# A mixture-of-experts decoder in which the experts' scatters add their rows to a copy of the residual in DRAM

## The chip, the cores and the metric

The kernel runs on one core of a Trainium2 chip. The metric is the device time of one execution in microseconds (us). Names used throughout: PE is TensorE (matmuls), PEld its weight loads, DVE is VectorE, ACT is ScalarE, POOL is GpSimd, SP is SyncE, which here only issues DMAs. POOL issues the indirect DMAs (gathers and scatters by a list of row numbers); all other transfers stand in one queue issued by SP, in program order.

## What is computed

Two decoder layers over 512 tokens of width 1024. A layer mixes tokens (two kinds of attention, unchanged here), normalizes, sends each token through 2 of 16 experts, adds, and normalizes again:

```python
x = layer_norm(DN_ALPHA * x + mix, ln1_g[l], ln1_b[l])            # "x1" below
ffn = grouped_moe(x, w_router, router_bias, exp_w_gate[l], exp_w_up[l], exp_w_down[l])
x = layer_norm(DN_ALPHA * x + ffn, ln2_g[l], ln2_b[l])

# in grouped_moe: combine[n, e] is the token's weight for expert e, zero for 14 of the 16
for e in range(N_EXPERTS):
    h = jax.nn.silu(xf @ exp_w_gate[e]) * (xf @ exp_w_up[e])
    y = y + combine[:, e:e + 1] * (h @ exp_w_down[e])
```

All is float32. `DN_ALPHA` is 4 ** 0.25, written `ALPHA` in the kernel. `layer_norm` adds `LN_EPS` to the variance.

## The kernel before

**Matmuls.** Tokens lie in four tiles of 128 rows (`NT` = 4). Each operand is split into a high and a low part (a CAST on ACT, then a subtraction on DVE, `split`, L484 and L495), and a product is three matmuls (`mm3`, L447). An expert reads 12 weight tiles of 128x1024 (512 KB each), so it has 12 such splits and 72 matmuls of 512 columns.

**Who sets the order.** Operations are recorded with a duration and dependencies, and `plan` lays them out on a model of the engines: it decides in which order each engine gets its instructions, which of 48 slots of 4 KB per partition (kind "s") or 56 small slots (kind "m") each tile takes, and when SP issues loads. The order is then fixed in the program: an instruction that waits holds up all behind it on its engine, SP's DMAs included. The model lets a POOL transfer end 0.65 us and the bytes' time and 0.9 us after its issue.

**Routing.** For each token tile, `out_proj` forms the first LayerNorm's output x1 and stores it to DRAM (`x1d`). `route_tile` picks the two experts and writes two entries (token number, weight) by scatters into a table in DRAM (`tabd`, L1151), row r of expert e for its r-th token; the first choice carries the token number, the second the number plus 512. `route_end` reads the first 128 rows of every expert back (`tb`) and computes from it the rows to gather (`gi`: numbers of 512 and more less 512).

**Experts.** `moe` runs expert after expert: `prep` gathers the expert's rows of x1 (POOL, L1179) and transposes them, `gate_up` makes 48 matmuls, `down` 24, and `put_rows` (L1185) scatters the weighted result into `yd`, a DRAM tile of 1024 rows: first choices in rows 0 to 511, second choices in the rest, so every row is written once and no scatter waits for another. The last expert's rows go nowhere by scatter; zeros are scattered for them at the start (tile z, L1342) and its result (yo and lo, its high and low part) is added in the second LayerNorm by matmuls with a one-hot matrix (`oh`). `overflow` is a branch (L1203) that every engine meets once in a layer, and whose body runs only where an expert has over 128 tokens; in this data none has, and the trace has no instruction of the body. Between the condition and the code that follows stand three copies of the body, 108 matmuls on PE.

**End of the layer.** For each tile x1 is loaded from `x1d` and both halves from `yd` (12 loads of 512 KB), two DVE operations of 128x1024 form ALPHA*x1 + y0 + y1, and `ln2` adds the last expert in PSUM (a matmul with the identity, then two with `oh`), takes mean and variance (tile 0 on DVE, the others on ACT), normalizes on DVE, stores the tile and, in the first layer, transposes and splits it for the next layer's projections. Loads of weights that follow in the program (ln2's, the next layer's `w_idx` and `w_main`) may be issued from the middle of expert 13 on (`R.after = mark`).

Of the kernel before, what the change touches and what calls it, by code (L numbers as in the profile page):

```python
# [11 lines left out]
F = mybir.dt.float32  # L12
FR = mybir.dt.float32r
BF = mybir.dt.bfloat16
I32 = mybir.dt.int32
# [7 lines left out]
P = 128  # L23
# [68 lines left out]
class Recorder:  # L92
# [82 lines left out]
    def plan(self):  # L175
# [109 lines left out]
        while done < len(self.ops):  # L285
# [69 lines left out]
            elif e == "POOL" and o.nbytes:  # L355
# [3 lines left out]
                o.end = dma_free + 0.9  # L359
# [176 lines left out]
THROTTLE = 3  # L536
# [7 lines left out]
def build(tc, x0, xT0, w_idx, w_main, w_br, w_out, w_exp, bgate, idxg, idxb,  # L544
          ln1g, ln1b, ln2g, ln2b, wrt, rbias, ln1c, hconst, tab0, out):
    nc = tc.nc
    with ExitStack() as ctx:
# [3 lines left out]
                 "k": ctx.enter_context(tc.tile_pool(name="k", bufs=1)),  # L551
                 "p": ctx.enter_context(tc.tile_pool(name="p", bufs=1, space=PSUM)),
# [3 lines left out]
        yd = tc.dram_tile([2 * S, D], F, name="yd")  # L556
# [4 lines left out]
        R.COUNT = {"s": NSLOT, "m": NSMALL, "k": 1, "p": 4, "a": 4}  # L561
# [22 lines left out]
        nc.gpsimd.iota(tokid, pattern=[[P, NT], [S, 2]], base=0, channel_multiplier=1)  # L584
# [74 lines left out]
        def rstd_of(mv):  # L659
            v, r = sm([P, 1]), sm([P, 1])  # L660
            C.ts(v, mv[:, 1:2], LN_EPS, None, OP.add)
            C.pow(r, v, nhalf)
            return r
# [4 lines left out]
        def norm_of(mv, bs):  # L668
            C.v("bn_aggr", mv, bs, n=12)
            return rstd_of(mv)  # L670
# [357 lines left out]
        def out_proj(l, mts, pair, xres, xtok, rw, rsum, rcon):  # L1028
# [26 lines left out]
            for t in range(NT):  # L1055
# [16 lines left out]
                C.dma(x1d[ts, :], r, P * 4096, wtok=[f"x1{t}"])  # L1072
                yield t, r, sc, scored, o
# [19 lines left out]
        def route_tile(t, rt, sc, scored, sels, oh0, xacc):  # L1093
# [44 lines left out]
            o2, ri = sm([P, 2, NE]), sm([P, 2], I32)  # L1138
            C.tt(o2, oh, pr[:, None, :NE].to_broadcast([P, 2, NE]), OP.mult)
            C.v("reduce_max", ri, o2, axis=AX.X, n=2 * NE)  # L1140
            ent, o3, w2, rw = sm([P, 2, 2], I32), sm([P, 2, NE]), sm([P, 2]), sm([P, 2])
# [5 lines left out]
            last = C.ts(ent[:, :, 1:2].bitcast(F), w2[:, :, None], rw[:, 1:2], None, OP.mult)  # L1147
# [12 lines left out]
        scatters, table_writes, picks, later, puts, written = [], [], [], [], [], []  # L1160

        def route_end(sels):
# [6 lines left out]
            tb, gi, gl = sm([P, NE, 2], I32), sm([P, NE], I32), sm([P, 2], I32)  # L1169
            o = C.dma(tb, tabd[0:P * NE, :].rearrange("(r e) w -> r e w", e=NE), P * 160, rtok=["tab0"])  # L1170
            o.deps.update(table_writes)
            C.ts(gi, tb[:, :, 0], float(S), float(-S), OP.is_ge, OP.mult)
            C.tt(gi, gi, tb[:, :, 0], OP.add)
            C.ts(gl[:, 0:1], gi[:, NE - 1:NE], float(S - 1), None, OP.min)
            return tb, gi, gl, mci
# [7 lines left out]
        def put_rows(idx, src, l, wait=()):  # L1183
            def fn():
                s_ = nc.gpsimd.indirect_dma_start(out=yd, out_offset=IOA(ap=real(idx), axis=0), in_=real(src), in_offset=None,  # L1185
                                                  bounds_check=2 * S - 1, oob_is_err=False)
                for x in puts:
# [423 lines left out]
```

## Time and profile before

| | us |
|---|---|
| median of 3 runs | 1546.22 (1542.68 to 1550.23) |
| the profiled execution | 1544.22 |
| its span in the trace | 1542.5 |
| PE busy in the span | 1477.8 (96%) |
| DVE busy | 1268.0 (82%) |
| ACT busy | 896.6 (58%) |
| POOL busy | 128.4 (8%) |
| DMA, mean over the span | 203 GB/s |

The trace is to be read by stage. Layer 1 takes the first 750 us or so: attention to 360, output projection and routing to about 450, the experts to about 750; layer 2 repeats this. The views used are the busy times in chosen stretches, the timeline of one engine (with the idle time before an instruction and what ended it, in brackets), the waits, and the views of one line of the code.

### The profile page before, as it was taken

The page shows a single profiled execution, that of the slowest core. Times are in us where ns is not written, and L with a number is a line of the kernel's source. Part 1 is how long each engine was busy: PE and PEld are TensorE (multiplying, and loading weights), DVE is VectorE, ACT ScalarE, POOL GpSimd, SP SyncE. Part 2 cuts the span into 40 slices and gives each one's busy share as a digit, 9 for nine tenths or more (in the row PEclk, how much of TensorE's full clock was granted, in tenths as well). Part 3 has the DMA queues.
Part 4 walks back from the last instruction along what each step waited for, and adds up shares of the span by engine and source line. Part 5 has one row for each costly group of instructions (what it writes and reads, how often), then busy time and mean ns, then how long its engine had stood idle before and what let it go on. Part 6 is the DMA issues. An engine that isn't in the chain of part 4 may idle for free. (4 is left out here: it accounts for less than half of the span.)

```text
span 1542.5 us, 21103 instructions
## 1 busy us (share of the span) xinstructions
PE 1477.8 (96%) x7188; PEld 1177.3 (76%) x7188; DVE 1268.0 (82%) x2321; ACT 896.6 (58%) x1459; POOL 128.4 (8%) x131
## 2 busy tenths in 40 slices
PE   8999999999989999999799999999999899999985
PEld 7877777777867788888487777777778578877874
DVE  5699995877687999989875999867766889899987
ACT  4335543674147888888433455346841578878773
POOL 0000000000131211111010000000001311111100
PEclk9999999999999999999899999999999899999998
DMA  7222113118778899999712211221287789999993
GB/s 222 72 84 67 57 55 96 56 42 304 268 249 307 328 349 343 335 337 332 297 69 67 85 55 55 83 82 55 68 316 254 260 309 337 347 331 323 351 328 147
DMA packets 92708, 313.15 MB, mean 203 GB/s; under 512 B 15757, under 2 KB 15885, under 8 KB 92592
## 3 DMA queue, kind: packets, MB, share of 16 engines
q1 hardware_dynamic: 83152, 294.88, 54.6%
q0 software_dynamic: 9440, 16.83, 3.0%
q8 instruction: 60, 0.98, 0.3%
q14 instruction: 56, 0.46, 0.1%
HBM read 302.19 MB, written 25.31 MB: 212 GB/s over the span
## 5 line engine op out<-in xcount | busy, mean ns | idle before, releaser
L447 PE MATMUL p<-s,s 128*128 128x512 f32 (+1 forms) x5192 | 1267.1, 397 | 30.0 <-DVE s L495 25.0
L447 PEld LDWEIGHTS p<-s,s 128*128 128x128 f32 x5192 | 950.2, 190 | 240.2 <-DVE s L495 25.6
L495 DVE TENSOR_TENSOR s<-s,s 128x1024 fp32r<-128x1024 f32 (+3 forms) x534 | 621.2, 1196 | 140.2 <-ACT s L484 106.8
L484 ACT CAST s<-s 128x1024 fp32r<-128x1024 f32 (+2 forms) x526 | 515.7, 1030 | 200.9 <-PE p L447 130.6
L495 DVE TENSOR_TENSOR s<-a,s 128x256 fp32r<-128x256 f32 (+3 forms) x386 | 168.8, 480 | 43.9 <-ACT s L484 40.4
L484 ACT CAST s<-a 128x256 fp32r<-128x256 f32 (+2 forms) x354 | 126.2, 414 | 123.7 <-PE a L445 107.1
L445 PE MATMUL a<-ident,s 128*128 128x128 f32 x888 | 132.3, 277 | 12.4 <-DMA s<-x1d,m 7.1
L445 PEld LDWEIGHTS a<-ident,s 128*128 128x128 f32 x888 | 106.2, 142 | 43.6 <-DVE s L495 11.4
L523 POOL TENSOR_TENSOR m<-m,nhalf 128x1 f32<-128x1 f32 x24 | 17.8, 743 | 902.1 <-DVE m L495 902.1
L480 ACT ACTIVATE s<-a 128x512 f32<-128x512 f32 (+3 forms) x156 | 61.8, 450 | 47.1 <-PE a L447 28.0
L484 ACT COPY s<-a 64x512 f32<-64x512 f32 (+1 forms) x48 | 27.8, 583 | 97.2 <-PE a L445 45.9
L487 ACT ACTIVATE s<-p,m 128x512 f32<-128x512 f32 (+1 forms) x64 | 44.2, 690 | 53.5 <-PE p L447 49.3
L464 PE MATMUL a<-s,s 64*128 64x384 f32 (+3 forms) x456 | 67.4, 351 | 0.0
L1179 POOL DMA_INDIRECT s<-x1d,m x30 | 42.9, 1430 | 265.6 <-PE p L447 248.3
L1185 POOL DMA_INDIRECT yd<-s,m x32 | 46.1, 1440 | 209.6 <-ACT s L487 189.6
L447 PEld LDWEIGHTS a<-s,s 128*128 128x128 f32 x360 | 57.1, 188 | 7.8 <-issue 2.4
L447 PE MATMUL a<-s,s 128*128 128x324 f32 (+4 forms) x360 | 62.4, 321 | 0.2
L464 PEld LDWEIGHTS a<-s,s 64*128 64x128 f32 x456 | 41.3, 185 | 27.6 <-issue 20.0
L495 DVE MAX8 m<-s 128x8 f32<-128x256 f32 (+2 forms) x96 | 53.5, 557 | 1.8
L495 DVE MATCH_REPLACE8 s<-m,s 128x256 f32<-128x256 f32 (+2 forms) x96 | 52.1, 543 | 0.0
L495 DVE TENSOR_TENSOR_SCAN s<-s 128x128 f32<-128x128 f32 (+3 forms) x64 | 51.1, 814 | 0.1
L484 ACT CAST s<-p 128x512 fp32r<-128x512 f32 x48 | 27.9, 588 | 35.6 <-DVE p L495 19.8
(108 smaller groups left out, 650.6 us busy)
## 6 DMA issues: line engine op xcount, KB each, us to landing
s<-in_w_exp SPq DMA_DIRECT2D x384, 512.0 KB
s<-in_w_main SPq DMA_DIRECT2D x79, 512.0 KB
s<-in_w_br SPq DMA_DIRECT2D x16, 512.0 KB
s<-in_w_out SPq DMA_DIRECT2D x16, 512.0 KB
s<-yd SPq DMA_DIRECT2D x16, 512.0 KB
x1d<-s SPq DMA_DIRECT2D x8, 512.0 KB
s<-x1d SPq DMA_DIRECT2D x8, 512.0 KB
s<-in_w_idx SPq DMA_DIRECT2D x8, 324.0 KB
```

The source lines that it names most:

```text
L445: self.nc.tensor.transpose(o, real(transpose[0]), transpose[1])
L447: self.nc.tensor.matmul(o, real(w), real(x), start=start and i == 0, stop=stop and i == len(terms) - 1)
L464: self.nc.tensor.matmul(real(o), real(t[i][0]), real(t[i][1]), start=i == 0, stop=stop and i == len(t) - 1)
L480: self.nc.scalar.activation(real(out), real(src), func, bias=real(bias), scale=real(scale), **kw)
L484: return self.r.add("ACT", 0.1 + self.psum(out, src) + self.n(out) * 0.833e-3, lambda: self.nc.scalar.copy(real(out), real(src)), [out], [ ...
L487: return self.r.add("ACT", 0.2 + self.n(out) * 0.833e-3, lambda: self.nc.scalar.mul(real(out), real(src), real(c)), [out], [src, c])
L495: getattr(self.nc.vector, method)(real(out), *[real(a) for a in args], **{k: real(x) for k, x in kw.items()}, **({} if accum is None else ...
L523: return self.r.add("POOL", 0.47, lambda: self.nc.gpsimd.tensor_tensor(real(out), real(a), e, OP.pow), [out], [a])
L1179: R.add("POOL", 1.04, lambda: nc.gpsimd.indirect_dma_start(out=real(dst), out_offset=None, in_=x1d, in_offset=IOA(ap=real(idx), axis=0), * ...
L1185: s_ = nc.gpsimd.indirect_dma_start(out=yd, out_offset=IOA(ap=real(idx), axis=0), in_=real(src), in_offset=None, bounds_check=2 * S - 1, o ...
```

## The change

- The result tile `yd` becomes `zd`, 512 rows. Each tile of x1 is stored twice, to `x1d` and to `zd` (four more stores of 512 KB in a layer), and `add_rows` in place of `put_rows` scatters with an addition in DRAM (`compute_op=OP.add`). The scatters are no longer declared independent: each waits until the one before it has landed, the first for the four stores.
- ALPHA is taken out: entries' weights are divided by ALPHA, and the second LayerNorm works on x1 + ffn/ALPHA with LN_EPS/ALPHA². At the end of a layer four loads from `zd` replace the twelve, and the eight DVE operations on them are gone.
- Both choices carry the plain token number; `gi` goes, the gathers take `tb` itself. The tile of zeros and its scatter go.
- The rows' numbers and the entries (`ri`, `ent`) get eight buffers of their own (kind "t") in place of shared small slots.
- Loads that follow the experts may be issued only behind the last expert load (`R.after = loads["last"]`).
- The three copies in the overflow body become one in a loop; 36 matmuls remain between the condition and what follows.
- In the planner's model a POOL transfer ends no earlier than 4.9 us (small) or 7.8 us (rows) after its issue.

```diff
-                o.end = dma_free + 0.9
+                o.end = max(dma_free + 0.9, t + ROWS[o.nbytes > P * 1024])
...
-THROTTLE = 3
+THROTTLE, ROWS = 3, (4.9, 7.8)
...
                 C.dma(x1d[ts, :], r, P * 4096, wtok=[f"x1{t}"])
+                written.append(C.dma(zd[ts, :], r, P * 4096, rtok=["y"]))
...
-            last = C.ts(ent[:, :, 1:2].bitcast(F), w2[:, :, None], rw[:, 1:2], None, OP.mult)
+            last = C.ts(ent[:, :, 1:2].bitcast(F), w2[:, :, None], rw[:, 1:2], 1.0 / ALPHA, OP.mult, OP.mult)
...
+        def add_rows(idx, src):
+            rows = R.add("POOL", 1.04, lambda: nc.gpsimd.indirect_dma_start(
+                out=zd, out_offset=IOA(ap=real(idx), axis=0), in_=real(src), in_offset=None,
+                bounds_check=S - 1, oob_is_err=False, compute_op=OP.add), reads=[idx, src], rtok=["y"], nbytes=P * 2048)
+            rows.deps.update(written[-NT:])
...
-                    for j in range(1, S // P):
...
+                    with tc.For_i(P * NE, S * NE, P * NE) as j:
...
-            z = s4([P, D])
-            R.add("POOL", 1.2, lambda: nc.gpsimd.memset(z.real(), 0.0), [z]).deps.add(routed)
-            put_rows(tb[:, NE - 1, 0:1], z, l)
...
-            R.after = mark
+            R.after = loads["last"]
...
-                a, y0, y1 = (s4([P, D]) for _ in range(3))
-                C.dma(a, x1d[ts, :], P * 4096, rtok=[f"x1{t}"]).deps.add(mark)
-                for j, y in ((0, y0), (1, y1)):
-                    C.dma(y, yd[j * S + t * P:j * S + (t + 1) * P, :], P * 4096, rtok=["y"]).deps.update(written)
-                R.bump -= 70
-                C.stt(a, a, ALPHA, y0, OP.mult, OP.add)
-                C.tt(a, a, y1, OP.add)
-                R.bump += 70
+                a = s4([P, D])
+                C.dma(a, zd[t * P:(t + 1) * P, :], P * 4096, rtok=["y"]).deps.update(written)
```

The first place is POOL at the start of layer 1's experts, before (tabd: the table, yd: the zeros' scatter, s<-x1d: gathers of experts 1 to 4):

```order
L1151 DMA tabd<-m_4363,m_4438 8192x2
L1185 DMA yd<-s_4429,m_4506 1024x1024
L1179 DMA s_4549<-x1d,m_4532 128x1024
L1179 DMA s_4562<-x1d,m_4532 128x1024
L1179 DMA s_4627<-x1d,m_4532 128x1024
L1179 DMA s_4757<-x1d,m_4532 128x1024
L1185 DMA yd<-s_4787,m_4506 1024x1024
```

The same place now:

```order
L1153 DMA tabd<-t_4368,t_4439 8192x2
L1179 DMA s_4552<-x1d,m_4517 128x1024
L1179 DMA s_4572<-x1d,m_4517 128x1024
L1179 DMA s_4653<-x1d,m_4517 128x1024
L1179 DMA s_4757<-x1d,m_4517 128x1024
L1184 DMA zd<-s_4786,m_4517 512x1024
```

Nothing stands between the table's scatters and the first gather any more, and the gathers read their row numbers from the table as loaded (m_4517, which the scatter reads too), not from a tile computed from it.

The second place is SP near the end of layer 1's experts, before (in_w_exp: expert weights, in_w_idx and in_w_main: layer 2's):

```order
L526 DMA s_7052<-in_w_exp 128x1024
L1024 DMA s_7071<-in_ln2g 128x1024
L1025 DMA s_7073<-in_ln2b 128x1024
L526 DMA s_7075<-x1d 128x1024
L526 DMA s_7077<-x1d 128x1024
L526 DMA s_7079<-x1d 128x1024
L526 DMA s_7081<-x1d 128x1024
L526 DMA s_7083<-in_w_idx 128x648
L526 DMA s_7088<-in_w_idx 128x648
L526 DMA s_7090<-in_w_idx 128x648
L526 DMA s_7206<-in_w_exp 128x1024
L526 DMA s_7224<-in_w_exp 128x1024
```

The same place now, from the last expert weights to the overflow branch:

```order
L526 DMA s_7152<-in_w_exp 128x1024
L526 DMA s_7171<-in_w_exp 128x1024
L1025 DMA s_7226<-in_ln2g 128x1024
L1026 DMA s_7230<-in_ln2b 128x1024
L526 DMA s_7232<-in_w_idx 128x648
L526 DMA s_7234<-in_w_idx 128x648
L526 DMA s_7238<-in_w_idx 128x648
L1198 TENSOR_LOAD m_4486
```

Before, eight expert loads follow the first of these other loads, with two more groups of w_idx and w_main among them; now all expert loads come first, and the fourth w_idx load, the first w_main load, the four zd loads and further w_main loads follow in this order behind the branch. At the start of the experts the queue changes too: two more expert loads stand ahead of the load of the table (`tb`).

The third place is DVE at the end of layer 1, from lo (the last expert's low part, two halves) on, before (s_7075 to s_7081: the four x1 tiles and the additions to them, m_7716: statistics of tile 0):

```order
L495 SCALAR_TENSOR_TENSOR s_7695<-p_7666,m_4506,s_7690 128x512
L495 TENSOR_TENSOR s_7075<-s_7075,s_7619 128x1024
L495 SCALAR_TENSOR_TENSOR s_7077<-s_7077,s_7623 128x1024
L495 TENSOR_TENSOR s_7077<-s_7077,s_7625 128x1024
L495 SCALAR_TENSOR_TENSOR s_7079<-s_7079,s_7627 128x1024
L495 BN_STATS m_7716<-p_7704 128x6
L495 TENSOR_TENSOR s_7079<-s_7079,s_7631 128x1024
L495 BN_STATS m_7716<-p_7706 128x6
L495 SCALAR_TENSOR_TENSOR s_7081<-s_7081,s_7633 128x1024
L495 BN_AGGR m_7730<-m_7716 128x2
L495 TENSOR_SCALAR m_7732<-m_7725 128x1
L495 TENSOR_TENSOR s_7081<-s_7081,s_7635 128x1024
```

The same place now (128x1024 with two s operands: splits of layer 2's w_main, loaded behind zd):

```order
L495 SCALAR_TENSOR_TENSOR s_7546<-p_7519,m_4517,s_7541 128x512
L495 BN_STATS m_7560<-p_7548 128x6
L495 TENSOR_TENSOR s_7566<-s_7517,s_7554 128x1024
L495 BN_STATS m_7560<-p_7551 128x6
L495 TENSOR_TENSOR s_7579<-s_7528,s_7564 128x1024
L495 BN_AGGR m_7583<-m_7560 128x2
L495 TENSOR_TENSOR s_7585<-s_7533,s_7573 128x1024
L495 TENSOR_SCALAR m_7590<-m_7583 128x1
```

Between lo and the normalizing of tile 0 stood seven additions of 128x1024; now three splits of the same size stand there, whose loads are the ones behind zd.

## Rows read from the trace of the kernel before

**Rows 1.** Busy time by stretch: length, PE, PEld, DVE, ACT, POOL; PEclk; DMA share; GB/s
```profile
400.00:500.00 100.00, 92.45 (x457) 71.99 (x456) 78.91 (x201) 47.61 (x63) 22.52 (x28) 0.95 0.76 266
500.00:720.00 220.00, 218.10 (x1027) 179.84 (x1026) 202.09 (x201) 182.99 (x220) 36.28 (x23) 1.00 0.95 339
720.00:780.00 60.00, 48.60 (x209) 35.45 (x208) 53.16 (x73) 36.60 (x63) 4.39 (x5) 0.91 0.77 281
...
1160.00:1260.00 100.00, 92.12 (x447) 71.77 (x446) 76.52 (x197) 44.00 (x59) 20.82 (x27) 0.95 0.81 279
...
1480.00:1542.50 62.50, 42.05 (x187) 32.19 (x185) 48.51 (x69) 29.34 (x51) 4.80 (x6) 0.90 0.59 216
```

**Rows 2.** PE's waits over the span: us in total, times, longest
```profile
PE a L445 <- DMA s<-x1d,m: 7.1, 3, 2.7
...
PE p L447 <- PEq L1203: 4.5, 1, 4.5
```

**Rows 3.** PE's timeline at the first gathered tiles, both layers: start, us, what
```profile
459.70 1.06 PE L445 MATMUL a<-ident,s 128*128 128x128 f32 x8 [1.90 <-DMA s<-x1d,m]
...
464.85 1.97 PE L445 MATMUL a<-ident,s 128*128 128x128 f32 x8 [2.70 <-DMA s<-x1d,m]
...
1224.84 1.06 PE L445 MATMUL a<-ident,s 128*128 128x128 f32 x8 [2.54 <-DMA s<-x1d,m]
```

**Rows 4.** POOL's timeline at the same places: zeros' scatters, first gather
```profile
451.50 1.41 POOL L1185 DMA_INDIRECT yd<-s,m  x1 [4.65 <-DMA m<-tabd]
454.14 1.25 POOL L1179 DMA_INDIRECT s<-x1d,m  x1 [1.23 <-DVE m L495]
...
1216.79 1.83 POOL L1185 DMA_INDIRECT yd<-s,m  x1 [5.17 <-DMA m<-tabd]
```

**Rows 5.** The view of line 1203, the overflow branch: ns min/median/max, first and last start
```profile
L1203 PEldq COMPARE_BRANCH  x2: 1425/3622/5820, 738.8 to 1495.9; - x2
L1203 DVEq COMPARE_BRANCH  x2: 56/64/72, 739.8 to 1496.5; - x2
```

**Rows 6.** PE's timeline at the end of layer 1: expert 15, then the second LayerNorm
```profile
733.11 0.98 PE L447 MATMUL p<-s,s 128*128 128x256 f32 x6 [0.97 <-DVE s L495]
...
744.10 7.36 PE L447 MATMUL p<-s,s 128*128 128x512 f32 x24 [2.68 <-DVE s L495]
754.59 3.64 PE L447 MATMUL p<-s,ident 128*128 128x512 f32 x4 [3.13 <-DVE s L495]
...
764.83 3.64 PE L447 MATMUL p<-s,ident 128*128 128x512 f32 x4 [2.99 <-DVE s L495]
```

**Rows 7.** ACT's timeline there: a split that waits for a load
```profile
733.60 1.84 ACT L484 CAST s<-s 128x1024 fp32r<-128x1024 f32 x2 [1.02 <-DMA s<-in_w_exp]
```

**Rows 8.** DVE by shape, 748 to 768 us: busy us, mean ns; the additions
```profile
L495 DVE SCALAR_TENSOR_TENSOR s<-s,s 128x1024 f32<-128x1024 f32 x4 | 4.9, 1217 | 0.0
L495 DVE TENSOR_TENSOR s<-s,s 128x1024 f32<-128x1024 f32 x4 | 4.9, 1216 | 0.0
```

**Rows 9.** Timeline at the end of layer 2: down of expert 15, additions, statistics
```profile
1512.14 5.74 PE L447 MATMUL p<-s,s 128*128 128x512 f32 x24 [0.92 <-DVE s L495]
...
1519.32 1.22 DVE L495 TENSOR_TENSOR s<-s,s 128x1024 f32<-128x1024 f32 x1
...
1522.79 1.22 DVE L495 TENSOR_TENSOR s<-s,s 128x1024 f32<-128x1024 f32 x1
...
1523.92 0.21 DVE L495 BATCH_NORM_AGGREGATE m<-m 128x2 f32<-128x12 f32 x1
```

**Rows 10.** The view of line 1185, the plain scatters: who waits for them, time to land
```profile
  ACT s L484: 10.9, 6
...
DMA to landing us min/median/max: 6.4/7.7/8.3
```

**Rows 11.** POOL's timeline: scatters of experts 13 and 14, layer 1
```profile
721.11 1.48 POOL L1185 DMA_INDIRECT yd<-s,m  x1 [16.98 <-ACT s L487]
...
727.30 1.25 POOL L1185 DMA_INDIRECT yd<-s,m  x1 [4.71 <-ACT s L487]
```

More of the change, by code (lines that the diff above doesn't have):

```diff
@@ L666, in half, with norm_of @@
             return slice(n * 512, (n + 1) * 512)
-        def norm_of(mv, bs):
+        def norm_of(mv, bs, eps=LN_EPS):
             C.v("bn_aggr", mv, bs, n=12)
-            return rstd_of(mv)
+            return rstd_of(mv, eps)
         def normalize(dst, src, g, b, mv, rstd):
@@ L1158, in route_tile @@
             return last
-        scatters, table_writes, picks, later, puts, written = [], [], [], [], [], []
+        scatters, table_writes, picks, later, written = [], [], [], [], []
         def route_end(sels):
@@ L1181, in gather @@
                 [dst], [idx], rtok=[f"x1{t}" for t in range(NT)], nbytes=P * (2048 if skip else 4096), allocs=also)
[L1183 to L1187, printed above, removed]
-                    tc.declare_no_dep(s_.ins, x.ins, reason="other rows of the result")
-                puts.append(s_)
-            rows = R.add("POOL", 1.04, fn, reads=[idx, src], rtok=["y"], nbytes=P * 2048)
-            rows.deps.update(wait)
+        def add_rows(idx, src):
[3 more added lines that the diff above has]
+            rows.deps.update(written[-NT:])
             written.append(rows)
@@ L1208, in body @@
                 hh, ht = hs[:, 0, :], hs[:, 1, :].rearrange("p (k t) -> p k t", k=4)
-                rest = []
                 def half_product(e, i, lhs, ps, first, last):
@@ L1240, in body, with moe @@
                             nc.scalar.mul(xg[:, n * 512:(n + 1) * 512], py, ot[:, 1:2].bitcast(F))
-                        s_ = nc.gpsimd.indirect_dma_start(out=yd, out_offset=IOA(ap=ot[:, 0:1], axis=0), in_=xg, in_offset=None,
-                                                          bounds_check=2 * S - 1, oob_is_err=False)
-                        for x in puts:
-                            tc.declare_no_dep(s_.ins, x.ins, reason="other rows of the result")
-                        rest.append(s_)
-                puts.extend(rest)
+                        nc.gpsimd.indirect_dma_start(out=zd, out_offset=IOA(ap=ot[:, 0:1], axis=0), in_=xg, in_offset=None,
+                                                     bounds_check=S - 1, oob_is_err=False, compute_op=OP.add)
             o = R.add("ALL", 0.3, fn, reads=[mci], rtok=[f"x1{t}" for t in range(NT)] + ["tab0", "y"], allocs=bufs)
             written.append(o)
-        def moe(l, tb, gi, gl, mci, loads, xacc, until, routed):
+        def moe(l, tb, gl, mci, loads, xacc, until, routed):
             def prep(e):
@@ L1265, in prep @@
                 last = e == NE - 1
-                gather(xg, gl[:, 0:1] if last else gi[:, e:e + 1], [xh, xl], not last)
+                gather(xg, gl[:, 0:1] if last else tb[:, e, 0:1], [xh, xl], not last)
                 transpose_tile(xg, dst)
@@ L1326, in whole @@
                     if n:
[L1327 removed]
+                        add_rows(tb[:, e, 0:1], yo)
                 if lo is None:
@@ L1395, in expert_loads @@
                         loads[e, i, h].buf.caps = caps
+            loads["last"] = R.ops[-1]
             return loads
@@ L1429, in ln2 @@
                         C.v("bn_stats", bs[:, n, :], ps[n], n=512)
-                    rstd, mean = norm_of(mv, bs), mv[:, 0:1]
+                    rstd, mean = norm_of(mv, bs, LN_EPS / ALPHA ** 2), mv[:, 0:1]
                 for n in range(2):
```

40 lines of the change are left out of this document (17 added, 23 removed).

## The prediction

> **What bounds the kernel now.** I read the busy times by stretch first [rows 1]. Among the experts (500 to 720 us) PE is busy for 218.1 of 220 us at full clock: nothing that eases DVE, ACT or DMA there can return more than the 1.9 us left, or some 4 us over both layers. The idle time of PE that the change can touch lies in four places: 7.6 us of 400 to 500 (routing and the first experts), 7.9 us of 1160 to 1260 (the same in layer 2), 11.4 us of 720 to 780 (end of layer 1) and 20.4 us of the last 62.5 us, of which the final normalizing and storing is a part that no edit removes. In these stretches the granted clock is 0.90 to 0.95 instead of 1.00. Then the waits [rows 2] and the timelines say what ended the idle time: gathered rows of x1 at the first experts [rows 3], the overflow branch of layer 2 [rows 2, 5], DVE at the ends of the layers [rows 6]. From 720 to 780 DVE is busy for 53.2 of 60 us while PE stands still for a fifth: there DVE sets the pace.
>
> **The start of the experts.** The zeros' scatter and `gi` stood between the table's landing and the first gather. In layer 1 the scatter started at 451.50, when the table had come, and the gather at 454.14, after 1.41 us of the scatter and 1.23 us of waiting for DVE's `gi`: 2.64 us [rows 4]. In layer 2 the scatter alone took 1.83 us. Both leave the chain, and the gathers behind it move up alike. PE waited 1.90 and 2.70 us for gathered tiles in layer 1, 2.54 us in layer 2 [rows 3], so the shift is all used: 2.6 + 1.8 = 4.4 us. Upper bound 7.1 us, all three waits, if the planner, which now knows that a gather takes over 7 us, also fills them with other matmuls; lower bound 0, if the table comes later because two more expert loads now stand ahead of it in SP's queue. The two small DVE operations of `gi` and the table buffers are worth tenths.
>
> The four new stores are 2 MB a layer, about 6 us of all DMA engines at the 339 GB/s of the next stretch; from 400 to 500 us the engines are 0.76 busy [rows 1], which leaves 24 us. I cost them at nothing; without that cover one store, 1.5 us, can stand ahead of the table or a gather in each layer: up to 3 us.
>
> **The experts.** ACT waited 10.9 us in all for result tiles still held by scatters [rows 10], because the planner took a scatter's end too early; it now plans with 7.8 us, near the median of 7.7. PE lost at most 1.9 us a layer there. I take 1 us for both layers; bounds -4 (an adding scatter holds its tile longer than planned) and +3.8. That each scatter waits for the one before costs nothing in the loop: an expert takes over 17 us of PE (72 of the matmuls of [rows 9], 24 in 5.74 us), a landing 7.7 us. Behind the waiting scatter on POOL's queue stand only the next gather and, at the end, the branch and the second LayerNorm's small power operation.
>
> **The overflow branch.** PE's branch took 1.4 us in layer 1, hidden, and 5.8 us in layer 2, of which PE stood idle for 4.5 us [rows 2, 5]; on DVE, whose body is short, it took 0.06 to 0.07 us. The jump is over 108 matmuls, each with its weight load, and will be over 36. I take 4.4 us of gain, as if PE's branch became like DVE's; bounds +4.5 and -4.5 (the long case in layer 1 too, now that the branch stands ahead of the up product's last matmuls). The Trainium skill (Runtime: NRT & Kernel Launch, "Instruction fetch mechanics") says that instructions come in blocks of 256 and that a taken branch whose target is outside the two blocks at hand must first fetch. The unequal 1.4 and 5.8 us agree with that; by it the shorter jump would miss less often, but could still. The same section calls runtime control flow expensive, which speaks against the new inner loop; as the body is never entered here, that would change nothing.
>
> **The end of layer 1.** Two parts. First, 13 other loads stood ahead of the last expert's weights in SP's queue and now stand behind them; ACT's splits waited for weights, 1.02 us of it at 733.60 [rows 7], and PE 0.97 us just before [rows 6]. I take 1.0 us. Second, the eight additions, 9.8 us of DVE [rows 8], go. Not all is won: between lo and the normalizing of tile 0 seven of them, 8.5 us, are replaced by three splits of w_main of the same length, 3.7 us, which were done earlier before. Tile 0, on which the next layer's first matmuls wait, comes 8.5 - 3.7 = 4.8 us sooner. Sum 5.8 us. PE's waits of 3.13 and 2.99 us at 754.59 and 764.83 [rows 6] are what this shortens. Lower bound 0 (the moved splits and their loads are late instead), upper bound the stretch's idle 11.4 us and its clock loss, 9% of 60 or 5.4 us: 16.8 us.
>
> **The end of layer 2.** The last products end at 1512.14 + 5.74 = 1517.88, the statistics of tile 0 at 1523.92; between them lie three additions, 1519.32 to 1522.79, at 1.22 us: 3.7 us [rows 9]. What is late next are PE's matmuls with the identity and with `oh`, for which the statistics wait as well, so I take 2 us; bounds 0 and 3.7.
>
> **The sum.** 4.4 + 1 + 4.4 + 5.8 + 2 = 17.6 us. Against the profiled execution, 1544.2 (span 1542.5 and 1.7 around it): 1526.6. It was 2.0 us under the median of the runs, 1546.2, so on that scale 1528.6; I say 1528.
>
> **Rivals.**
>
> (a) *The adding scatters land late.* The end of a layer now hangs on a chain: scatter 13, wait for its landing, scatter 14, landing, loads of `zd`, the identity matmuls. Nothing in the trace shows an addition in DRAM. The nearest row is the plain scatter, 6.4 to 8.3 us [rows 10]; an addition reads the rows it writes, so below 6.4 is excluded. With scatter 13 at 721.11 [rows 11] and a landing time A, the first `zd` tile is there at 721.1 + 2A + about 3 us for a load. It is wanted when the last products end, at 751.5 before (744.10 + 7.36) [rows 6] and about 748 after. That gives A = 12 us as the point from which it decides; in my sum A is about 8. Beyond it each us costs 2 us a layer, 4 in all: the gain is eaten at A = 12 + 17.6/4 = 16.4 us, and at three times the plain landing, 23 us, the time is 1528 + 44 = 1572. For it speaks that two landings and the loads are serial where before nothing was; against it that only some 64 rows of 4 KB a scatter are moved. The Trainium skill (DMA: Bandwidth & Descriptors, "Rules for kernel authors") asks for exactly this wait between two accumulating transfers of the same bytes, and prices neither; by its fit for a transfer from GpSimd, 2.0 us and the bytes, A would be an estimated 2.6 us for a plain scatter, and the measured 7.7 us decides.
>
> (b) *The branch stays slow*: no gain there, 4.4 us less: 1533; or layer 1 also pays: 1537.
>
> (c) *The end of layer 1 gives it back*: the moved w_main loads stand behind `zd` in SP's queue and their splits in the middle of tile 0's statistics on DVE. If they are late, DVE waits where it added: 5.8 us less, 1534; with (b) 1539.
>
> (d) *The clock comes back.* In the four stretches the mean granted clock is 0.90 to 0.95 [rows 1], so it stood at the lower level, 1.2 GHz, for 10 to 20% of the time, and only there, where PE has gaps; if the gaps close, the 5.4 us at the end of layer 1 and some 5 us of the two starts follow, and tile 0 gains more than its own chain: about 10 us more, 1518.
>
> (e) *Nothing measurable*: PE's order among the experts moves with the planner's new landing times; if that loses as much as the rest wins, 1540 to 1546.
>
> **How the numbers follow.** Forecast (1523 to 1532): 0.42. (d) 0.20. (b) or (c) alone 0.18. (b) with (c), or (e): 0.12. (a): 0.08, of which half ends above the time before. The range leaves out (a) and the far ends of (d) and (e): 1512 to 1542. A difference under 0.5%, 7.7 us, is about what a measurement of this kernel cannot tell from none; faster than that means below 1538.5: the forecast, (d), and (b) or (c) alone are 0.80, less a little of the last that reaches over the line: 0.78. Slower: half of (a) and the losing end of (e): 0.07. Within: 0.15.
>
> **What would show it.** Right: no wait of PE for x1d at the first experts, the first gather starting as the table lands; a branch on PE of 0.1 us in both layers; in the end of layer 1 at least 5 us less idle time of PE and no DVE operation of float32 128x1024 with two operands; landings of the adding scatters of 7 to 10 us. Wrong: PE or ACT waiting for `zd` or for a scatter; SP held up by scatter 14 so that ACT waits for w_main; a branch of several us again. The sum would be wrong altogether if PE lost time inside 500 to 720 us, where it has none to win.

## The result, and the profile after

| | kernel before | changed kernel |
|---|---|---|
| median of 12 runs each, us | 1543.17 (1539.05 to 1551.39) | 1535.49 (1531.65 to 1544.44) |
| profiled execution, us (its span) | 1544.22 (1542.5) | 1539.54 (1537.7) |

The ratio is 0.9950, 95% interval 0.9934 to 0.9966: faster, by 7.7 us (5 to 10). The time lies in the range that was given, 1512 to 1542 us, and it is a gain, as forecast; but the forecast was a gain of 17.6 us. Over half of it is missing, and the runs below were made to find it.

PE runs the same 7188 matmuls in both kernels, so the start of the n-th in the two traces tells where the time went. The order within a stage differs; at the stages' borders the comparison is sound.

| n-th matmul | before | after | difference | in between |
|---|---|---|---|---|
| 2150 | 433.6 | 434.2 | +0.6 | attention, layer 1 |
| 2350 | 485.9 | 486.2 | +0.3 | first experts, layer 1: 0.3 won |
| 2650 | 551.6 | 550.3 | -1.2 | experts: 1.5 won |
| 2700 | 562.9 | 567.7 | +4.8 | experts: 6.1 lost at one place |
| 3450 | 722.7 | 725.1 | +2.5 | experts: 2.3 won |
| 3800 | 807.1 | 802.3 | -4.8 | end of layer 1: 7.3 won |
| 5700 | 1187.9 | 1184.8 | -3.1 | attention, layer 2: 1.7 lost |
| 6000 | 1263.6 | 1260.3 | -3.3 | first experts, layer 2: 0.2 won |
| 7000 | 1479.4 | 1473.7 | -5.7 | experts: 2.4 won |
| last | 1528.1 | 1522.8 | -5.3 | end of layer 2: 0.5 lost |

The busy times by stretch answer [rows 1] (length; PE, PEld, DVE, ACT, POOL; PE's clock, DMA share, GB/s):

```profile
400.00:500.00 100.00, 93.33 (x461) 73.35 (x460) 78.87 (x200) 47.43 (x62) 21.18 (x26) 0.95 0.82 287
500.00:720.00 220.00, 217.34 (x1015) 179.71 (x1014) 200.61 (x196) 181.73 (x219) 41.98 (x22) 0.98 0.97 337
720.00:780.00 60.00, 50.81 (x246) 39.95 (x245) 49.08 (x83) 40.31 (x72) 6.77 (x6) 0.97 0.69 227
```

From 720 to 780 PE is busy 2.2 us longer, at a clock of 0.97 instead of 0.91, and DVE 4.1 us less. From 500 to 720 PE lost what it hardly had to lose: its clock fell to 0.98 there.

**The start of the experts** ([rows 3, 4]): SP's queue, POOL and PE at the first gathers (start, us, what, in brackets the wait ahead of it).

```profile
440.69 9.93 SPq L526 DMA_DIRECT2D s<-in_w_exp  x5
451.25 0.33 SPq L526 DMA_DIRECT2D m<-tabd  x1
...
455.00 1.94 POOL L1179 DMA_INDIRECT s<-x1d,m  x1 [8.36 <-DVE m L495]
1215.98 1.34 POOL L1179 DMA_INDIRECT s<-x1d,m  x1 [8.27 <-PE p L447]
...
462.90 1.94 PE L445 MATMUL a<-ident,s 128*128 128x128 f32 x8 [1.68 <-DMA s<-x1d,m]
```

The zeros' scatter is gone, but the first gather of layer 1 starts at 455.00 (454.14 before). The table's load went out at 451.25, as SP's next after five expert loads that end at 450.62; before it went at 449.06. By the semaphores in the two traces it was not those loads that it waited for last: the last table scatter, issued at 445.68, landed at 451.1, after 5.4 us, where before one issued at 445.89 landed after 3.0. The load itself then took 2.9 us to land instead of 1.7. These two links became 3.6 us longer in layer 1 and 2.3 us in layer 2 (there 6.0 and 2.8 us instead of 4.9 and 1.6), more than the 2.64 and 1.83 us that were taken out. In layer 2 the gather waited last for PE, but only 0.4 us longer than for the table.

**The experts of layer 1.** POOL, ACT and PE around the place where 6.1 us went:

```profile
540.28 7.45 POOL L1184 DMA_INDIRECT zd<-s,m  x1 [5.03 <-ACT s L487]
556.21 2.94 ACT L484 CAST s<-s 128x1024 fp32r<-128x1024 f32 x3 [6.64 <-DMA zd<-s,m]
557.30 0.50 PE L447 MATMUL p<-s,s 128*128 128x512 f32 x1 [1.81 <-ACT s L484]
558.56 9.79 PE L447 MATMUL p<-s,s 128*128 128x512 f32 x29 [0.76 <-DVE s L495]
```

A scatter issued at 540.28 had landed only at 556.2, 15.9 us later, 7.45 of them on POOL. The slot of its result tile had been given to a split of weights; ACT waited 6.64 us for it, and PE for ACT. Two stretches show that this place is the whole loss (columns as above):

```profile
556.00:570.00 14.00, 11.94 (x45) 9.49 (x46) 11.31 (x10) 12.53 (x16) 2.05 (x1) 0.76 0.79 254
570.00:720.00 150.00, 150.00 (x713) 125.27 (x712) 139.55 (x138) 125.50 (x151) 25.01 (x15) 1.00 0.99 345
```

PE stood still for 1.81 + 0.76 = 2.6 us, and behind that its clock was at the lower of its two levels for a while (0.50 from 558 to 564): 29 matmuls took 9.79 us, 0.34 us each, where 24 take 5.72 us, 0.24 each, at the end of layer 2 (below). From 570 on PE has no gap, though ACT goes on waiting for scatters, up to 2.0 us at a time. The scatters as a group, answering [rows 10] (ns min/median/max; who waited, us and times):

```profile
L1184 POOL DMA_INDIRECT zd<-s,m x30: 1585/1794/7452, 485.6 to 1490.9; - x30
...
  ACT s L484: 17.0, 10
  DVE s L495: 12.4, 3
...
DMA to landing us min/median/max: 8.1/9.2/9.6
```

Landing is 9.2 us where the plain ones had 7.7 and the planner has 7.8. The view knows the landing of only 6 of the 30 (of 10 of 32 before), and the late one is not among them. Of the 29 us that ACT and DVE waited, 6.64 are the late scatter, and 9.6 are two waits at the ends of the layers that the next rows put down to the branch.

**The branch**, the view of its line, answering [rows 5] (ns min/median/max, first and last start):

```profile
L1199 POOLq EVENT_SEMAPHORE  x8: 17/43/4467, 731.9 to 1496.2; - x8
L1199 PEldq COMPARE_BRANCH  x2: 323/338/352, 728.9 to 1486.9; - x2
...
L1199 POOLq COMPARE_BRANCH  x2: 53/53/53, 731.4 to 1491.1; - x2
...
L1199 POOLq INC_SWDGE_SEM  x2: 948/1318/1687, 738.7 to 1496.3; - x2
```

The timelines of DVE and PE at the ends of layer 1 and of layer 2 ([rows 6, 9]):

```profile
739.72 1.23 DVE L495 TENSOR_TENSOR s<-s,s 128x1024 fp32r<-128x1024 f32 x1 [3.15 <-DMA zd<-s,m]
741.33 3.48 PE L447 MATMUL p<-s,s 128*128 128x256 f32 x18 [3.87 <-DVE s L495]
760.60 1.98 PE L447 MATMUL p<-s,ident 128*128 128x512 f32 x4 [2.46 <-DVE s L495]
...
1498.12 3.68 DVE L495 TENSOR_TENSOR s<-s,s 128x1024 fp32r<-128x1024 f32 x3 [6.45 <-DMA zd<-s,m]
1499.40 3.36 PE L447 MATMUL p<-s,s 128*128 128x256 f32 x14 [5.12 <-DVE s L495]
1506.91 5.72 PE L447 MATMUL p<-s,s 128*128 128x512 f32 x24
1512.47 1.88 PE L447 MATMUL p<-s,ident 128*128 128x512 f32 x4
1516.18 0.21 DVE L495 BATCH_NORM_AGGREGATE m<-m 128x2 f32<-128x12 f32 x1
```

PE's branch fell from 5.8 to 0.35 us. In its place PE now waits 5.12 us for DVE, and DVE 6.45 us. The profile names a scatter as DVE's releaser; the rows of the branch say more. Scatter 14 had to wait for scatter 13's landing and went out at 1490.92. POOL meets the branch behind it, at 1491.1, waits 4.47 us in one semaphore instruction for scatter 14's landing (the semaphore is the one that this scatter raises, for the last time at 1496.1), and closes its side with INC_SWDGE_SEM, which ends at 1496.3 + 1.69 = 1498.0. The semaphore that DVE waits for is raised at 1497.9, within that instruction, and DVE starts at 1498.12. In layer 1 the same: 738.7 + 0.95 = 739.6, DVE at 739.72. By the code, the body of the branch reserves five of the common slots, and the last splits of weights may take them only afterwards.

### The profile page after: what moved, and what is told of

Same layout as the page of the kernel before. It is cut to its first block, busy times and chain, and to the rows that moved or that the text cites. A ratio compares the mean times of both kernels' runs of the same rounds, so it can differ in the third digit from the quotient of the medians.

```text
span 1537.7 us, 21018 instructions
## 1 busy us (share of the span) xinstructions
PE 1475.2 (96%) x7188; PEld 1178.9 (77%) x7188; DVE 1249.5 (81%) x2301; ACT 896.6 (58%) x1459; POOL 142.4 (9%) x127
## 5 line engine op out<-in xcount | busy, mean ns | idle before, releaser
L495 DVE TENSOR_TENSOR s<-s,s 128x1024 fp32r<-128x1024 f32 (+2 forms) x526 | 612.1, 1195 | 152.4 <-ACT s L484 112.3
L480 ACT ACTIVATE s<-a 128x512 f32<-128x512 f32 (+3 forms) x156 | 61.9, 450 | 46.0 <-PE a L447 27.5
L1184 POOL DMA_INDIRECT zd<-s,m x30 | 61.1, 2035 | 199.8 <-ACT s L487 167.4
```

What stands on the lines that cost most here:

```text
L480: self.nc.scalar.activation(real(out), real(src), func, bias=real(bias), scale=real(scale), **kw)
L495: getattr(self.nc.vector, method)(real(out), *[real(a) for a in args], **{k: real(x) for k, x in kw.items()}, **({} if accum is None else ...
L1184: rows = R.add("POOL", 1.04, lambda: nc.gpsimd.indirect_dma_start(out=zd, out_offset=IOA(ap=real(idx), axis=0), in_=real(src), in_offset=None,
```

## The experiments

Each ratio is to the kernel before on the same chip; in the table it is also multiplied by 1543.2, to have one scale.

| run | ratio (95% interval) | us on one scale |
|---|---|---|
| changed kernel | 0.9950 (0.9934 to 0.9966) | 1535.5 |
| loop_alone | 0.9988 (0.9968 to 1.0008) | 1541.3 |
| late_alone | 1.0006 (0.9985 to 1.0026) | 1544.1 |
| before_branch_earlier | 0.9964 (0.9946 to 0.9983) | 1537.6 |
| plain_scatter | 0.9854 (0.9826 to 0.9881) | 1520.7 |
| own_slots | 1.0071 (1.0046 to 1.0097) | 1554.2 |
| table_early | 0.9952 (0.9930 to 0.9975) | 1535.8 |
| loads_not_late | 0.9966 (0.9946 to 0.9986) | 1538.0 |
| branch_earlier | 0.9836 (0.9808 to 0.9865) | 1517.9 |
| landing_9_6 | 0.9853 (0.9828 to 0.9878) | 1520.5 |
| both | 0.9822 (0.9799 to 0.9845) | 1515.7 |
| both_unrolled | 0.9858 (0.9835 to 0.9880) | 1521.3 |
| both_plain | 0.9832 (0.9808 to 0.9856) | 1517.3 |

**Is it the addition?** The scatter without its addition:

```diff
-                bounds_check=S - 1, oob_is_err=False, compute_op=OP.add), reads=[idx, src], ...
+                bounds_check=S - 1, oob_is_err=False), reads=[idx, src], ...
```

> The changed kernel with scatters that overwrite the rows of zd instead of adding to them (so the output lacks the sum: of each row only one expert's result is left); each still waits for the one before, and order, slots and plan are the same. Theory: the time lost among the experts of layer 1 (6 us) and at the end of layer 2 (some 4 us) comes from the longer stay of an adding scatter, 9.2 us to landing against 7.7 and 1.8 us on POOL against 1.2, which holds the result tile's slot beyond the planned 7.8 us; without the addition the waits of ACT and DVE for scatters fall from 29 us to below 10 and the time to 1526 to 1530. Rival: it is the chain of waits between the scatters, with POOL's queue behind it, that holds the slots, not the addition: then the waits stay and the time is 1533 to 1537.

Measured 0.9854, 14.8 us below the changed kernel on one scale. The scatters of this kernel, as above:

```profile
L1184 POOL DMA_INDIRECT zd<-s,m x30: 1007/1218/1677, 484.6 to 1479.4; - x30
...
  DVE s L495: 6.6, 3
  ACT s L484: 1.2, 1
...
DMA to landing us min/median/max: 6.2/7.7/9.5
```

The waits for scatters fell from 29 us (and one of 9.2 us on POOL) to 7.8, as the theory said, so the chain of waits alone is not it; the time is below the theory's 1526 to 1530. It is also below the 1528 of the forecast: in this plan the missing gain is the price of the addition. The scatter that took 7.45 us on POOL takes 1.68 here, and the 6.1 us at that place are back. (Layer 2 computes on other data here, so its scatters carry other rows.) What the price is paid for was still open: slots, another wait, or the addition's own cost.

**Slots of their own for the result tiles.**

```diff
-                yo = s4([P, D], F if e < NE - 1 else FR)
+                yo = R.buf("y", [P, D], F) if e < NE - 1 else s4([P, D], FR)
...
-NSLOT, NSMALL = 48, 56
+NSLOT, NSMALL = 46, 56
```

> The changed kernel with two buffers of their own for the experts' result tiles, taken from the 48 common slots (46 left), so that a split of weights or of activations can never get a slot whose content a scatter still reads. Theory (held slots): no wait of DVE or ACT's splits for a scatter is left, the 6 us lost among the experts of layer 1 and some 4 us at the end of layer 2 come back: 1526 to 1529 us. Rival: the losses come from the planner's new order and from the clock, not from the slots: 1533 to 1537, or up to 1540 if two common slots fewer make the loads late.

Measured 1.0071, slower than both kernels: neither expectation. The trace parts it in two. The busy times among the experts of layer 1 (columns as above):

```profile
500.00:720.00 220.00, 220.00 (x1050) 183.91 (x1049) 205.22 (x201) 186.54 (x227) 39.33 (x23) 1.00 0.99 351
```

DVE's timeline at the end of layer 1, and below it POOL's closing instruction in the view of the branch's line:

```profile
747.13 3.68 DVE L495 TENSOR_TENSOR s<-s,s 128x1024 fp32r<-128x1024 f32 x3 [10.02 <-DMA zd<-y,m]
```

```profile
L1200 POOLq INC_SWDGE_SEM  x2: 948/1318/1687, 746.1 to 1518.2; - x2
```

PE has no gap among the experts: there the theory of the held slots holds, though no scatter was late there either (at most 2.04 us on POOL). But 10 us were lost in the attention of layer 1, long before an expert, and 11 in that of layer 2, with two common slots fewer, and at the ends DVE waited 10.0 and 7.6 us "for a scatter" though no split can get a scatter's slot any more. It starts 0.1 us after the end of POOL's closing instruction (746.08 + 0.95 = 747.03). That made the branch, not the slot, the suspect at the ends.

**The branch one expert earlier, and the longer landing in the plan.**

```diff
-AHEAD, LNB, NOW = 1, 150, 0
+AHEAD, LNB, NOW = 2, 150, 0
```

> The changed kernel with the overflow branch one expert earlier (AHEAD 2 instead of 1: after the products of expert 12 instead of 13), nothing else. Theory: at the end of each layer the splits of the last weights take slots that the body of the branch had reserved, and wait until POOL has passed the branch; POOL comes to it only behind scatter 14, which waits for the landing of scatter 13, then waits itself for scatter 14's landing and closes the branch with an instruction of 1.0 to 1.7 us (in layer 2 until 1498.0, when DVE starts again; in layer 1 until 739.6, likewise). One expert earlier there are 17 us of products for this: PE's waits of 5.1 us in layer 2 and 3.9 us in layer 1 go, the last split waits for no scatter: 1535.5 - 7 = 1527 to 1530 us. Rival: the splits wait for result tiles held by the scatters themselves, wherever the branch stands: 1534 to 1537, and DVE or ACT still wait 5 us or more for a scatter at the end of layer 2.

```diff
-THROTTLE, ROWS = 3, (4.9, 7.8)
+THROTTLE, ROWS = 3, (4.9, 9.6)
```

> The changed kernel with 9.6 us instead of 7.8 us as the planned time to landing of a row scatter, above the longest that was measured there (9.6, median 9.2). Theory: what is lost among the experts are slots given out while an adding scatter still reads them, because the plan takes its end 1.4 us too early; with 9.6 us the waits of ACT and DVE for scatters fall from 29 us to below 12, and the time to 1529 to 1532 (the end of layer 2, where the branch sets the pace, stays as it is). Rival: those waits are mostly off PE's path, the 6 us lost at 558 us are one late scatter (7.45 us on POOL) that no plan foresees: the waits fall, the time stays at 1533 to 1537.

Measured 0.9836 and 0.9853: 17.6 and 15.0 us below the changed kernel, over twice what was expected of each. With the branch earlier, no wait of over 1.3 us is left on PE at the ends of the layers, where 3.87 and 5.12 us stood, while ACT still waits 15.8 us for scatters among the experts. POOL's closing instruction, and PE at the same two places as above:

```profile
L1199 POOLq INC_SWDGE_SEM  x2: 908/1278/1647, 717.4 to 1464.0; - x2
```

```profile
739.80 2.42 PE L447 MATMUL p<-s,s 128*128 128x256 f32 x18 [0.52 <-DVE s L495]
756.55 1.98 PE L447 MATMUL p<-s,ident 128*128 128x512 f32 x4 [1.25 <-DVE s L495]
...
1486.70 2.06 PE L447 MATMUL p<-s,s 128*128 128x256 f32 x15 [0.51 <-DVE s L495]
```

By the n-th matmuls of the two traces 6.5 us are won at the end of layer 1 and 6.9 at the end of layer 2; the waits alone are 9.0, and PE's clock, with fewer gaps, is 1.00 instead of 0.97 from 720 to 780. With 9.6 us planned nothing waits for a scatter among the experts, where 7.6 us are won in layer 1 and 3.9 in layer 2, but POOL's closing instruction still holds DVE at the end of layer 1 (733.18 + 0.95 = 734.13), with a wait of 5.90 us. In layer 2 scatter 14 goes out at 1477.9 there, and the closing, from 1483.2, is in time: 6.8 us are won at that end too, so this run is no test of the slots alone. The busy times among the experts of layer 1, DVE's timeline at its end, and the closing instruction, all of the kernel with 9.6 us planned:

```profile
500.00:720.00 220.00, 220.00 (x1046) 183.77 (x1045) 205.59 (x204) 187.31 (x226) 41.77 (x23) 1.00 0.98 349
```

```profile
734.23 1.23 DVE L495 TENSOR_TENSOR s<-s,s 128x1024 fp32r<-128x1024 f32 x1 [5.90 <-DMA zd<-s,m]
```

```profile
L1199 POOLq INC_SWDGE_SEM  x2: 948/1318/1687, 733.2 to 1483.2; - x2
```

So there are two losses, a slot among the experts and the branch at the ends. Is the first the 1.4 us by which the plan is short, or the one late scatter, as the rival has it? The traces speak for the scatter. It took over 7 us in three kernels, this one, branch_earlier and loads_not_late, and only there does PE stand still at this place (2.3 to 2.9 us). In table_early (below), with 7.8 us planned, no scatter took over 2.6 us; ACT and DVE still wait 5.1 us for scatters among the experts of layer 1, and PE loses half a microsecond:

```profile
500.00:720.00 220.00, 219.49 (x1035) 181.71 (x1034) 204.88 (x203) 185.36 (x223) 39.12 (x23) 1.00 0.98 345
```

A plan of 9.6 us would not have covered 15.9. In the order that it gave the late scatter did not occur, so the rival's mechanism stands, although its time, 1533 to 1537, was wrong.

> The changed kernel with the branch one expert earlier and 9.6 us as the planned landing of a row scatter. Theory: two separate losses, slots of result tiles among the experts (7.7 us in layer 1, some 3 us in layer 2) and POOL's late closing of the branch at the ends (5.9 us of DVE at the end of layer 1 even with 9.6 us planned), so that the two repairs add up in part: 1511 to 1516 us against 1519.6 and 1521.5 for each alone. Rival: both repairs remove the same wait, that of the splits of the last weights for the last scatters: 1518 to 1522.

Measured 0.9822, the best of all: 27.5 us (24 to 31) under the kernel before, 20 under the changed one. Its interval overlaps those of each repair alone, so that they add up is seen in the trace (PE busy for 219.85 of 220 us among the experts of both layers, the closing instructions at 709.5 and 1458.0, long before the ends) and not shown by the times. What comes next is the first `zd` load: PE waits 3.3 us for it at the end of layer 1, a wait that the changed kernel does not have.

> The kernel with both repairs (branch one expert earlier, 9.6 us planned), with scatters that overwrite the rows of zd instead of adding to them (so the output lacks the sum). Theory: the addition itself costs only where a plan or a queue does not allow for its later landing; with the plan allowing for it, taking it away gives under 3 us, at the very ends, where two landings of 1.5 us more stand in the chain: 1515 to 1519 against 1519. Rival: the addition costs by itself, through POOL's longer issue or DRAM traffic that slows the weight loads: 1508 to 1514.

Measured 0.9832 against 0.9822: no difference that intervals of 0.0024 to either side can tell, that is, none of over 4 us. Landing falls from 9.6 to 7.5 us. **With this plan the addition costs nothing measurable. Most of what it cost in the changed kernel, 15 us, were the waits of others: ACT's for one late scatter, and DVE's for POOL, which came through the branch only behind two landings.**

**The branch.** The slot loop alone in the kernel before:

```diff
-                    for j in range(1, S // P):
+                    with tc.For_i(P * NE, S * NE, P * NE) as j:
```

> The kernel before with the slot loop of the overflow body alone (108 matmuls in the skipped body become 36), all else untouched. Theory: PE's branch in layer 2 falls from 5.8 us to the 0.3 us that it takes in the changed kernel, and the 4.5 us that PE stood idle for it are gained whole, since nothing else is late there in the kernel before: 1543.2 - 4.4 = 1538.8 us, ratio 0.997. Rival: the branch only covered another wait (DVE's splits of the last weights), the branch gets short and the time stays within 1 us of 1543.

Measured 0.9988, a gain of 1.9 us that can't be told from none. PE's branch is short, and yet (the view of the branch's line, and ACT's timeline at the end of layer 2):

```profile
L1203 POOLq INC_SWDGE_SEM  x2: 964/1346/1727, 733.5 to 1499.2; - x2
L1203 PEldq COMPARE_BRANCH  x2: 236/290/344, 741.1 to 1495.7; - x2
```

```profile
1500.91 3.89 ACT L484 CAST s<-s 128x1024 fp32r<-128x1024 f32 x4 [1.91 <-DMA yd<-s,m]
```

POOL closes the branch at 1499.18 + 1.73 = 1500.91, and there ACT starts. In the kernel before ACT started at 1501.84, held by PE's branch; POOL's closing, which ended at 1500.54, was hidden 1.3 us behind it. About that, and not 4.4 us, is what the loop alone can give.

> The kernel with both repairs (branch one expert earlier, 9.6 us planned), with the body of the branch unrolled again as in the kernel before: 108 matmuls to jump over instead of 36. Theory: with POOL's closing off the path, PE's branch is bare: if it takes 1.4 to 5.8 us as in the kernel before, the time is 3 to 9 us above the kernel with both repairs and the slot loop. Rival: PE has enough queued ahead of the branch for its jump to be hidden: within 2 us.

Measured 1523.7 us against 1519.0 on the same chip, ranges of the runs 1522.7 to 1526.9 and 1515.2 to 1521.2: the loop is worth 4.8 us once POOL's closing is out of the way. PE's branch over 108 matmuls again took 5.6 us once, now in layer 1 (the view of the branch's line, and PE's waits: total, times, longest):

```profile
L1199 PEldq COMPARE_BRANCH  x2: 333/2985/5637, 715.2 to 1466.8; - x2
```

```profile
PE p L447 <- PEq L1199: 3.8, 1, 3.8
```

> The kernel before with the branch one expert earlier, unrolled body and all else as before. Theory: there too POOL closes the branch late (in layer 2 at 1500.5 us, 7.6 us after scatter 14), and with it PE's branch of 5.8 us, if it is long again, lies in the same place of PE's queue but one expert earlier; PE loses its 4.5 us there all the same, while the wait at the end goes: no change to 3 us of gain, 1540 to 1545. Rival: POOL's closing was the whole cause also of PE's long branch: 4 to 8 us of gain, 1535 to 1539.

Measured 0.9964: 5.6 us (2.6 to 8.3) of gain, more than the theory's 3; but PE still lost 3.6 us to its branch (5.9 us long), so the rival is wrong as well. By the n-th matmuls the gain is at the end of layer 1, 11.7 us, against 5.9 lost just ahead of it, where PE's branch now stands; the end of layer 2 gains nothing. In the kernel before, too, the place of the branch cost the end of layer 1.

**The other parts.**

> The changed kernel with the planned landing time of the table scatters (4.9 us) taken back to the kernel before's rule; the 7.8 us of the row scatters stay. Theory: the table's load stands again two expert loads earlier in SP's queue and goes out at about 449 us instead of 451.25, the first gather starts about 2 us earlier in layer 1, and the gain of the start of the experts that is missing appears: 1532 to 1534 us. Rival: the loads that then wait behind the table's load land later, and PE waits for split weights instead of gathered rows: 1535 to 1538.

Measured 0.9952: no change. The table's load now goes out without expert loads in its way, but the last table scatter itself is 1.9 us later in this plan (447.63 against 445.68), the first gather starts at 455.47, and in layer 2 PE waits 5.2 us for a gathered tile. The queue's order is not what keeps the gain away, and the rival's mechanism, PE waiting for weights, isn't seen either. What the traces have in common is the landing of the last table scatter of layer 1: 2.1 to 3.0 us after its issue in the kernel before and the three made from it, 5.0 to 5.9 in the changed kernel and the nine made from it, 5.1 here. Which part of the change makes it longer is not shown. The 6.1 us among the experts are not lost in this kernel; against the changed kernel it loses 3.5 us in the experts just ahead of that place and 4.8 at the end of layer 1, and so comes out the same.

> The changed kernel with the loads of the next layer and of the last LayerNorm free to go as early as before (from the mark three experts before the end, not after the last expert load): this part of the change undone alone. Theory: the weights of the last expert come later again behind 13 other loads, ACT's splits wait about 1 us for them at the end of layer 1, and the time is 1 us longer, 1535 to 1538. Rival 1: the late loads gave most of the 8.3 us that the end of layer 1 gained, and it is lost: 1540 to 1544. Rival 2: the late loads cost time, since the splits of w_main (DVE, 3 of 1.2 us) now lie in the middle of the normalizing: 1529 to 1533.

> The kernel before with the late loads alone (loads of the next layer only after the last expert load), additions and plain scatters as they were. Theory: about 1 us of gain at the end of layer 1 (0.97 us of PE, 1.02 us of ACT for the last expert's weights), and against it the splits of w_main fall behind the eight additions on DVE, which is busy 53 of 60 us there: 1541 to 1545, no change that can be measured. Rival: the order of the loads is what gave the end of layer 1 its gain in the changed kernel: 1535 to 1539.

Measured 0.9966 and 1.0006. Without the late loads the changed kernel is 2.5 us slower, with intervals that overlap. In its trace the end of layer 1 has lost all of its gain: PE waits 8.44 us there for DVE, which starts 0.1 us after POOL's closing instruction again, so the loss is that of the branch as much as that of the loads. Alone they change nothing; but in that trace PE's long branch struck in both layers (two waits, 11.3 us), which may cover a gain. Their worth stays open.

## Why the prediction was right in sign and half short

By its own terms, with the gain in the profiled executions from the table of matmuls:

- **The start of the experts**: 4.4 forecast, 0.5 measured. The scatter and `gi` left the chain, but "both leave the chain, and the gathers behind it move up alike" failed: the links ahead of the gather, the landing of the last table scatter and that of the table's load, became 3.6 and 2.3 us longer. The lower bound had the table come later, by two expert loads in SP's queue; table_early took those away, and the scatter's landing stayed at 5.1 us.
- **The experts**: +1 forecast, in layer 1 a loss of 2.3 (6.1 lost at one place, the rest won), in layer 2 2.4 won. The cause of the loss is the lower bound's: "an adding scatter holds its tile longer than planned". The step that failed is that 7.8 us planned, near the median of the plain scatters, was enough. What it failed on was one scatter that landed after 15.9 us; the usual 9.2 us cost PE nothing from 570 to 720. Its sign of a wrong sum, PE losing time inside 500 to 720 us, came true.
- **The branch**: 4.4 forecast, nothing in the changed kernel. The mechanism was right (0.35 us measured; 4.8 us in both_unrolled against both), and what was late next was missed. The prediction looked at PE's and DVE's branch and not at POOL's, and it named the branch as standing behind the waiting scatter on POOL's queue without a price. The price was 5.12 us of PE in layer 2 and 3.87 in layer 1.
- **The end of layer 1**: 5.8 forecast, 7.3 measured, in spite of the 3.87 us. The clock rose with it, 0.97 instead of 0.91, which is the start of rival (d). With the branch earlier it is 1.00.
- **The end of layer 2**: 2 forecast. The statistics of tile 0 do come 2.5 us sooner after the last product (1516.18 - 1512.63 = 3.55 us against 6.04), but the last matmul comes no sooner after it: PE's products for the other tiles set the end, as the prediction said of "what is late next", and then it still took 2.
- **The attention of layer 2** lost 1.7 us, at a lower clock of PE (0.97 instead of 1.00 from 1100 to 1160). No term had it, and its cause is open. It comes and goes: plain_scatter and both have it too, branch_earlier and landing_9_6 do not.

The sum is 0.3 - 2.3 + 7.3 - 1.7 + 0.2 + 2.4 - 0.5 = 5.7, less 0.6 lost before, so 5.1 in the profiled executions (4.8 in the span) and 7.7 in the medians. A second estimate that failed is the point from which rival (a) decides. It was put at a landing of 12 us, where the first `zd` tile would be late; but in the changed kernel PE never waits for a `zd` load. (The 3 us that it allowed for that load were too few: the first one at the end of layer 1 took 4.9 us to land, and 6.5 in the kernel with both repairs, where PE does wait.) The branch stood nearer: two landings in a row held up POOL, and 6.7 and 7.4 us in layer 1, 8.5 and 5.2 us in layer 2, were enough. Its mechanism, the chain of landings, was right, its place and its price were not.

That the time fell into the range is in part luck. 1535.5 us is outside the forecast's 1523 to 1532 and near the 1533 to 1539 of rivals (b) and (c), but neither of these happened: PE's branch was short, and the end of layer 1 gave back nothing. Losses that had no price came to about the same sum.

The Trainium skill (Runtime: NRT & Kernel Launch, "Instruction fetch mechanics") was cited for jumps that miss; both_unrolled agrees with it, since a jump over 108 matmuls cost 0.3 us in one layer and 5.6 in the other, and the jump over 36 never more than 0.35 in any run here. A fetch itself is in no trace.

## What to carry to other kernels

A transfer that is made to wait for another puts the whole queue of its engine behind that landing: before pricing the wait at nothing, list what stands there, branches and their closing included, and who waits for those. When a planner hands out buffers by a transfer's landing time, look at the latest landing and not only at the median: 9.2 us instead of 7.8 cost PE nothing among the experts of layer 1, one scatter of 15.9 us cost 6 us. And a stall that is removed is worth only the distance to the next one, on any engine: look at all engines' sides of a branch, not at the longest alone.

## What was not expected of the hardware

An indirect scatter that adds takes 1.8 us on POOL and 9.2 us to land, where the plain one takes 1.2 and 7.7, for the same sizes (landing by 6 and 13 of 30 scatters; by 19 in landing_9_6 it is 9.2 as well, and by all 30 in both_plain 7.5). To close a branch that was not taken, POOL needed an instruction of 0.91 to 1.73 us, 3 to 10 us after the branch, when the scatter issued just ahead of it had landed (727.6 to 731.4 in the kernel before, 699.9 to 709.5 in the kernel with both repairs).

One scatter of layer 1 took 7.45 us on POOL in the changed kernel, 7.44 in branch_earlier and 7.45 in loads_not_late, which share the plan up to there; in landing_9_6 none took over 2.3. It started with 6.0 us of DVE splits still to come that followed each other without a gap, and ended 1.5 us after DVE had turned to PSUM. In the kernel before, the one long scatter (5.26 us, at 505.28) had 4.4 us of them ahead. Over all runs eleven scatters began with more than 4 us of such splits to come; ten took 4.1 to 7.5 us, and one, with 5.6 us of them ahead in the kernel with both repairs, 2.5. One with 3.9 us took 1.9, and many with splits ahead that left gaps of 0.1 us took 1.4 to 2.9 us, among them the same scatter in plain_scatter (1.68). So the splits are a strong suspect and no more; no run was made on it.

The Trainium skill (SBUF — State Buffer, "Who interferes with whom") says that a VectorE instruction with two inputs in SBUF gets in the way of GpSimd's reads there, and infers that making descriptors is not hit by it. The ten long scatters speak against that inference, the 2.5 and 1.9 us for it.
